# Four up-projection groups of an MLP as seven block products, with the MLP's program order computed from a task plan

## The chip, the cores and the metric

The kernel runs on one core of one Trainium2 chip. The metric is device time in microseconds (us), the median of several executions. Five engines work side by side, each going through its own instructions in program order and waiting on semaphores for the others: TensorE (PE in the profile, with its weight loads shown apart as PEld), VectorE (DVE), ScalarE (ACT), GpSimd (POOL) and SyncE (SP). SP issues nearly all loads and stores; POOL issues the DMAs that add into their destination.

## The reference, cut to what matters

One decoder layer on 512 tokens of width 1024: two mixing branches, a merge, and then a squared-ReLU MLP of width 4096. The change is in the MLP, the last lines:

```
x  = x + jnp.einsum('bsd,de->bse', merged, w_out[l])
h2 = rmsnorm(x, norm_mlp_g[l])
up = jnp.square(jax.nn.relu(jnp.einsum('bsd,df->bsf', h2, w_up[l])))
x  = x + jnp.einsum('bsf,fd->bsd', up, w_down[l])
```

## The kernel before, in words

**Precision.** Every large product is made of three: both operands are split into a high part (ACT copies the float32 value into the rounded type, `fp32r`) and a low part (DVE subtracts the high part from the value), and `high*high + high*low + low*high` goes into one PSUM bank. A weight block of 128 x 1024 so costs one load on SP, one ACT cast (tile `whi`) and one DVE subtraction (tile `wlo`). There are five pairs of `whi`/`wlo` buffers, four in the pool `wp` and one in `fin`, so the weights can lead the products by at most five blocks (`slots`, `weight_pair`, L80 to 84). Four buffers hold raw blocks: two of tag `rx` and two of tag `wraw` (`load`, L1036).

**The MLP's work.** The list of its products starts at L1004, the loop over them at L1284. `w_up` is cut into 8 groups of 512 hidden columns and `w_down` into 8 matching pieces; the work goes in 4 chunks `d`. Chunk `d` does up group `2d`, up group `2d+1`, then the two halves `(d, 0)` and `(d, 1)` of the down projection. The list `steps` holds the products in this order. A group is done in one of two ways:

- **Plain** (`"pl"`: groups 0, 1, 3, 5 and 7): four weight blocks `b0`, `b2`, `b1`, `b3`, each used by 8 x 3 matmuls of 128 x 512, 96 matmuls in all.
- **Seven products** (`"up"`: groups 2, 4, 6, and every down half, `"dn"`): the 2 x 2 block product is done with seven block products `M1` to `M7` instead of eight (a Strassen-Winograd form), in the order M1, M5, M6, M2, M7, M3, M4. Each product is 24 matmuls of 128 x 256, 168 in all. Sums of weight blocks and of activation blocks are needed for it, and sums of results behind it.

The weight sums are made in two ways. For groups 2, 4 and 6 they are computed long before the MLP with adding DMAs on POOL and kept in DRAM (`weight_sums`, L281, tiles `up2M...`), so these groups load seven finished blocks. For the down halves four blocks are loaded, DVE adds twice in place (`plus`, L1063, `raw<-raw`: for M5 and M6), and POOL adds twice with a DMA (in `cast_lo`, L1086, `raw<-raw`: for M7 and M4). The text calls a group whose sums are made on the spot a *grown* group.

**Banks.** A seven-product group uses three PSUM banks X, Y and Z. M1, M6, M7 and M4 all go into Y, one onto the other, with a copy or an addition of the state by ACT or DVE between them; M5 and M3 share Z. So one product lies between two products of the same bank, and what takes the first one's result has to be done in that time.

**After the products.** `plain_out` and `up_out` (L1157 to 1228) make relu and square on ACT, the four sums of activation blocks on DVE (`total`), and high and low parts of the seven forms (tiles `us`). `down_out` (L1230) adds each down product into `x` on DVE; in the last chunk it scales and stores the rows.

**The order by hand.** Matmuls, DVE, ACT and POOL instructions are chained in the order in which the program emits them (`InOrder`, L59). The loop over `steps` emits a product, then one weight step (`ahead`, L1104: the subtraction of one block and the cast of the next). Work behind a product is delayed with `later(us, f)` (L1120) and let go by `tick` (L1123), with hand-written delays such as `later(4.9, ...)`. At the start of each down half `(d, 0)` stands one extra matmul of 64 columns, whose result the next one overwrites:

```
if kind == "dn" and a[1] == 0 and p == "M1" and k == 0:
    I.matmul((b[0] if isinstance(b, tuple) else b)[:, :64], hi[:, 0, :P], forms[2 * a[0]][:, 0, f, 0, :64], start=True, stop=True)
```

**Lines in the profile.** Nearly every instruction goes through `InOrder` and so has line L67; the tile names tell the work apart: `acc<-h,...` is an up product, `acc<-us,...` a down product, `x<-acc,x` the addition of a down product, `q<-acc,...` the work behind an up product, `fs` the activation sums, `us<-...` their high and low parts.

Of the kernel before, what the change touches and what calls it, by code (L numbers as in the profile page):

```python
# [19 lines left out]
P = 128  # L20
# [17 lines left out]
def tile_block(ctx: ExitStack, tc: tile.TileContext, x, w_in, w_rga, w_rgx, w_pa, w_pr, w_o,  # L38
# [935 lines left out]
    def merged(j):  # L974
        def done(ps):
            q = fin.tile([P, 4, 256], F32, tag="q", name="q")
            d = h2[:, :, j]
            for c in range(2):
                t = 2 * j + c
                V.tensor_tensor(out=x2[:, t, :], in0=ps[c], in1=x2[:, t, :], op=ALU.add)  # L980
                A.activation(q[:, 2 * c:2 * c + 2], x2[:, t, :].rearrange("p (u s) -> p u s", u=2), AF.Copy, scale=smt[:, C_G2 + t:C_G2 + t + 1])
            for c in range(2):
                hi_part(d[:, :, 2 * c:2 * c + 2], q[:, 2 * c:2 * c + 2])
                lo_part(d[:, :, 2 * c:2 * c + 2], q[:, 2 * c:2 * c + 2])
            def sums():
                fs = fin.tile([P, 4, 256], F32, tag="fs", name="fs")
                sums_to(fs, *(q[:, m] for m in (1, 0, 3, 2)))
                hi_part(d[:, :, 4:8], fs)
                late.append(lambda: lo_part(d[:, :, 4:8], fs))
# [11 lines left out]
    FORM = {"M1": 0, "M4": 1, "M2": 2, "M5": 3, "M6": 4, "M7": 5, "M3": 6}  # L1001
    ORDER7 = ("M1", "M5", "M6", "M2", "M7", "M3", "M4")
    every = range(4)
    steps = []  # L1004

    def products(kind, a, order=ORDER7, first=3, lead=()):
        steps.extend((kind, a, p, q) for q in (range(first), range(first, 4)) for p in lead)
        steps.extend((kind, a, p, every) for p in order if p not in lead)

    I = InOrder(nc.tensor)  # L1010
# [10 lines left out]
    uses = {"M1": ("b0",), "M5": ("b0", "b1"), "M6": ("b0", "b3"), "M2": ("b2",), "M7": ("b1", "b3"), "M3": ("b3",), "M4": ("b2", "b0")}  # L1021
    loads = []
    for kind, a, p in ops:
        if kind == "pl":
            loads.append(((kind, a, p), w_up[a, int(p[1])]))
        elif kind == "up":
            loads.append(((kind, a, p), w_up[a, int(uses[p][0][1])] if p in ("M1", "M2", "M3") else summed[a // 2 - 1][p]))
        else:
            b = w_dn[2 * a[0] + a[1]].rearrange("a b p c -> (a b) p c")
            for q in (0, 1, 3, 2) if a[1] else (0, 2, 1, 3):  # L1030
                if p == "M1":
                    loads.append((("dn", a, f"b{q}"), b[q]))
    raw, dead, units, half = {}, set(), [], []
    n_load, n_free, n_low = [0], [0], [0]

    def load():  # L1036
        while n_load[0] < min(len(loads), n_free[0] + 4):
            n = n_load[0]
            if n >= 2 and len(wb.raw) < len(wb.reqs):
                break  # L1040
            what, src = loads[n]
            t = fin.tile([P, 4, 256], F32, tag="rx", name="raw", bufs=2) if n % 4 < 2 else wp.tile([P, 4, 256], F32, tag="wraw", name="raw", bufs=2)
            nc.sync.dma_start(t, src.rearrange("p (k c) -> p k c", k=4))
            raw[what] = t
            n_load[0] += 1

    def drop(what):
        dead.add(what)
        while n_free[0] < n_load[0] and loads[n_free[0]][0] in dead:
            n_free[0] += 1  # L1050
        load()

    def can_cast():
        load()
        n = len(units)
        if n == len(ops) or slots[0] == 0:
            return False
        kind, a, p = ops[n]
        return all((kind, a, q) in raw for q in (uses[p] if kind == "dn" else (p,)))

    added, cast = set(), set()

    def plus(n):  # L1063
        if n in added or n >= len(ops):
            return
        kind, a, p = ops[n]
        if kind == "dn" and p in ("M5", "M6"):
            x, y = (raw.get((kind, a, q)) for q in uses[p])
            if x is None or y is None:
                return  # L1070
            V.tensor_tensor(out=x, in0=x, in1=y, op=ALU.add)
        added.add(n)

    def cast_hi():
        n = len(units)
        plus(n)
        slots[0] -= 1
        kind, a, p = ops[n]
        src = raw[kind, a, uses[p][0] if kind == "dn" else p]
        own = n % 5 == 4  # L1080
        hi, lo = weight_pair((0 if own else 64) if kind != "pl" else 192 if own else 0, fin if own else None)
        A.copy(hi, src)
        units.append((hi, lo))
        half.append((hi, lo, src, ops[n]))

    def cast_lo(more=True):  # L1086
        hi, lo, src, (kind, a, p) = half.pop(0)
        V.tensor_tensor(out=lo, in0=src, in1=hi.bitcast(F32), op=ALU.subtract)
        n_low[0] += 1
        if kind != "dn":  # L1090
            drop((kind, a, p))
        elif p in ("M2", "M6"):
            cast.add((a, p))
            if {(a, "M2"), (a, "M6")} <= cast:
                G.dma_start(raw[kind, a, "b2"], raw[kind, a, "b0"], accum_op=ALU.add)
                drop((kind, a, "b0"))
        elif p in ("M7", "M3", "M4"):
            drop((kind, a, uses[p][0]))
        if kind == "dn" and p == "M5":
            G.dma_start(raw[kind, a, "b1"], raw[kind, a, "b3"], accum_op=ALU.add)  # L1100
        if not half and more:
            plus(len(units))

    def ahead():  # L1104
        if half:
            cast_lo()
        if can_cast():
            cast_hi()

    finished, freed = set(), [0]  # L1110

    def finish(o):
        finished.add(o)
        while freed[0] < len(ops) and ops[freed[0]] in finished:
            freed[0] += 1
            slots[0] += 1

    clk, due = [0.0], []

    def later(us, f):  # L1120
        due.append((clk[0] + us, f))

    def tick(us):  # L1123
        clk[0] += us
        for d in sorted(due, key=lambda d: d[0]):
            if d[0] <= clk[0]:
                due.remove(d)
                d[1]()

    two = lambda b: b.rearrange("p (u s) -> p u s", u=2)  # L1130
    forms, quads = [None] * 8, {}

    def begin(n):
        if n % 2:
            t = fin.tile([P, 7168 + 64], F32R, tag="us1", name="us")[:, 48:48 + 7168]
        else:
            t = hp.tile([P, 7168], F32R, tag="hT", name="us")
        forms[n] = t.rearrange("p (r f h s) -> p r f h s", r=2, f=7, h=2)

    def squared(q, a, b, src=None):  # L1140
        A.activation(q[:, a:b], q[:, a:b] if src is None else src, AF.Relu)
        A.activation(q[:, a:b], q[:, a:b], AF.Square)

    def part(n, which, f0, f1, src, u=slice(0, 2)):
        return lambda: which(forms[n][:, :, f0:f1, u], src)

    def total(n, fs, *ms, u=slice(0, 2)):
        q = quads[n][0][:, :, u]
        fs = [f[:, :, u] for f in fs]
        for m in ms:  # L1150
            x, y, op = ((q[:, 0], q[:, 2], ALU.subtract), (fs[0][:, 0], q[:, 1], ALU.subtract), (q[:, 1], q[:, 0], ALU.subtract), (q[:, 3], fs[0][:, 1], ALU.add))[m]
            V.tensor_tensor(out=fs[m // 2][:, m % 2], in0=x, in1=y, op=op)

    def rests():
        return hp.tile([P, 2, 2, 256], F32, tag="tail", name="fs"), fin.tile([P, 2, 2, 256], F32, tag="fs", name="fs")

    def up_out(n, p, X, Y, Z):  # L1157
        if p == "M1":
            begin(n)
            snap = fin.tile([P, 2, 256], F32, tag="fs", name="snap")  # L1160
            A.copy(snap, two(Y))
            quads[n] = fin.tile([P, 4, 2, 256], F32, tag="q", name="q"), snap
            return
        q, snap = quads[n]
        if p == "M5":
            A.copy(q[:, 2], two(Z))
        elif p == "M6":
            A.copy(q[:, 3], two(Y))
        elif p == "M2":
            V.tensor_tensor(out=q[:, 1], in0=two(X), in1=snap, op=ALU.add)  # L1170
            later(1.0, lambda: squared(q, 1, 2))
# [19 lines left out]
    def plain_out(n, c, u, ps):  # L1191
# [12 lines left out]
        if u == 0:  # L1204
            quads[n] = q, rests()
# [44 lines left out]
    def sums2():  # L1250
        split(s2[:, 0], s2[:, 1], ssq)
# [134 lines left out]
```

## Time and profile before

| what | value |
|---|---|
| time, median of 3 runs | 851.39 us (850.86 to 852.13) |
| span of the profiled execution | 849.3 us |
| PE, PEld, DVE, ACT, POOL busy | 843.4, 762.0, 632.1, 460.7, 97.0 us |
| first MLP product starts, last one ends | 523.80, 845.37 us |
| granted TensorE clock | 1.000 |

The span runs from the first to the last instruction of one profiled execution. A matmul's row shows its start and a modelled duration that overlaps the next one's; the pace of PE is read from the distance of starts, or from how long a stage with a known number of matmuls takes. The same holds for DVE and ACT to a smaller degree: instructions back to back start a little sooner than the shown duration says. A figure in brackets behind a row is the idle time in front of it, with what ended it.

### The profile page before, as it was taken

Reading aid. Unit: us, or ns where it says so; the run is one execution under the profiler, and the core shown is the slowest. Engines: PE = TensorE matmul, PEld = TensorE weight load, DVE = VectorE, ACT = ScalarE, POOL = GpSimd, SP = SyncE. Lnnn points to the kernel's source line nnn. Section 1 sums busy time; section 2 is a strip of 40 time slices with the busy share of each in tenths; the row PEclk is TensorE's granted clock in tenths of the full one; section 3 lists DMA queues with packets and bytes.
Section 4 is the critical chain, followed back from the end, with each engine's and each line's share of the span. In section 5 each row is a group of like instructions: output and inputs, shape, how many; then the busy total and the mean of one; then the engine's idle time right before and its main releaser. Section 6 shows DMA issues by size and latency. Waiting matters only on the chain.

```text
span 849.3 us, 13700 instructions
## 1 busy us (share of the span) xinstructions
PE 843.4 (99%) x5395; PEld 762.0 (90%) x5395; DVE 632.1 (74%) x1061; ACT 460.7 (54%) x719; POOL 97.0 (11%) x124
## 2 busy tenths in 40 slices
PE   9999999999999999999999999999999999999998
PEld 7899999999888888888888888889999998999898
DVE  6766788888877246878875767698786858876797
ACT  7445465655655336577662456563466356545641
POOL 0041232313211101111111000000000000000000
PEclk9999999999999999999999999999999999999999
DMA  5356332343332346686656651414843565356354
GB/s 202 123 158 205 106 94 71 94 124 88 87 93 77 99 151 189 188 231 175 187 152 188 223 215 45 157 38 137 248 149 77 150 221 149 124 153 198 98 149 124
DMA packets 40016, 121.85 MB, mean 143 GB/s; under 512 B 4864, under 2 KB 9672, under 8 KB 39952
## 3 DMA queue, kind: packets, MB, share of 16 engines
q1 hardware_dynamic: 31152, 92.65, 33.2%
q0 software_dynamic: 8800, 28.33, 15.2%
q8 instruction: 42, 0.69, 0.3%
q14 instruction: 22, 0.18, 0.1%
HBM read 102.05 MB, written 11.05 MB: 133 GB/s over the span
## 4 chain that ended last, share of the span: by engine, by line
PE 94%; DVE 4%; ACT 1%; issue 1%; DVEq 0%
PE acc L67 38%; PE acc L137 15%; PE acc L138 15%; PE acc L139 15%; PE at L593 2%; PE at L137 2%; PE at L138 2%; PE at L139 2%; PE at L629 1%; DVE wlo L67 1%; PE at L527 1%; PE at L666 1%; DVE pe L67 1%; DVE hT L67 0%; DVE xT L67 0%
## 5 line engine op out<-in xcount | busy, mean ns | idle before, releaser
L67 PE MATMUL acc<-h,whi 128*128 128x512 f32 (+1 forms) x656 | 156.5, 332 | 0.0
L67 PE MATMUL acc<-us,whi 128*128 128x256 f32 (+1 forms) x900 | 154.1, 277 | 0.1
L67 DVE TENSOR_TENSOR wlo<-wraw,whi 128x1024 fp32r<-128x1024 f32 (+2 forms) x86 | 96.9, 1148 | 71.9 <-ACT whi L67 68.7
L67 ACT CAST whi<-raw 128x1024 fp32r<-128x1024 f32 x97 | 99.7, 1049 | 91.4 <-DVE raw L67 41.1
L67 PEld LDWEIGHTS acc<-us,whi 128*128 128x128 f32 x900 | 136.1, 188 | 0.6 <-DVE x L67 0.3
L67 DVE TENSOR_TENSOR wlo<-raw,whi 128x1024 fp32r<-128x1024 f32 x97 | 117.5, 1218 | 15.4 <-ACT whi L67 15.2
L67 PE MATMUL acc<-us,wlo 128*128 128x256 f32 x448 | 124.0, 277 | 0.0
L67 PEld LDWEIGHTS acc<-h,whi 128*128 128x128 f32 x656 | 110.9, 188 | 12.3
L67 PE MATMUL acc<-h,wlo 128*128 128x256 f32 (+1 forms) x328 | 108.9, 332 | 0.0
L67 ACT CAST whi<-wraw 128x1024 fp32r<-128x1024 f32 (+2 forms) x86 | 82.5, 982 | 48.5 <-DMA wraw<-in_w_in_dram 31.7
L137 PE MATMUL acc<-whi,hT 128*128 128x256 f32 x384 | 108.4, 282 | 0.0
L138 PE MATMUL acc<-wlo,hT 128*128 128x256 f32 x384 | 107.3, 279 | 0.2 <-DVE wlo L67 0.2
L67 PEld LDWEIGHTS acc<-us,wlo 128*128 128x128 f32 x448 | 84.1, 188 | 0.0
L137 PE MATMUL acc<-hT,whi 128*128 128x512 f32 x208 | 81.7, 393 | 0.0
L139 PE MATMUL acc<-hT,wlo 128*128 128x512 f32 x208 | 81.0, 390 | 0.0
L139 PE MATMUL acc<-whi,hT 128*128 128x256 f32 x288 | 80.3, 279 | 0.0
L138 PEld LDWEIGHTS acc<-wlo,hT 128*128 128x128 f32 x384 | 72.4, 189 | 0.6 <-DVE wlo L67 0.4
L137 PEld LDWEIGHTS acc<-whi,hT 128*128 128x128 f32 x384 | 72.4, 188 | 0.5 <-issue 0.2
L67 ACT ACTIVATE pe<-pe,nm 128x128 f32<-128x128 f32 (+3 forms) x64 | 35.6, 558 | 65.9 <-DVE nm L67 65.9
L67 PEld LDWEIGHTS acc<-h,wlo 128*128 128x128 f32 x328 | 61.6, 188 | 6.3
L138 PE MATMUL acc<-hT,whi 128*128 128x512 f32 x156 | 60.8, 390 | 0.0
L67 POOL TENSOR_TENSOR rs<-ms,mhalf 128x8 f32<-128x8 f32 (+1 forms) x25 | 39.4, 1579 | 187.2 <-DVE ms L67 187.2
(210 smaller groups left out, 1680.2 us busy)
## 6 DMA issues: line engine op xcount, KB each, us to landing
wraw<-in_w_in_dram SPq DMA_DIRECT2D x54, 512.0 KB, 3.6
raw<-in_w_dn_dram SPq DMA_DIRECT2D x32, 512.0 KB, 4.1
raw<-in_w_up_dram SPq DMA_DIRECT2D x29, 512.0 KB, 4.3
sum<-in_w_up_dram POOLq DMA_DIRECT2D x18, 512.0 KB, 5.7
raw<-raw POOLq DMA_DIRECT2D x16, 512.0 KB, 4.6
wraw<-in_w_pa_dram SPq DMA_DIRECT2D x8, 512.0 KB, 4.6
wraw<-in_w_pr_dram SPq DMA_DIRECT2D x8, 512.0 KB, 3.6
wraw<-in_w_o_dram SPq DMA_DIRECT2D x8, 512.0 KB, 4.7
```

Source lines behind the costliest of these rows:

```text
L67: ins = f(*a, **k)
L137: T.matmul(o, l[0], r[0], start=first, stop=False)
L138: T.matmul(o, l[0], r[1], start=False, stop=False)
L139: T.matmul(o, l[1], r[0], start=False, stop=last)
L527: T.transpose(out=ps[:, t * P:(t + 1) * P], in_=qn[t // 2][:, c0:c0 + P], identity=ident)
L593: T.matmul(lg[c][:, :N], qT[:, c, i * P:(i + 1) * P], qk[h % 2, z][:, c, :N], start=z == 1, stop=z == 2)
L629: T.transpose(out=tp[:, b * P:(b + 1) * P], in_=st[s][:, b * P:(b + 1) * P], identity=ident)
L666: T.matmul(ps[:, t:t + 1], sq[:, t * P:(t + 1) * P], ones, start=True, stop=True)
```

## The change

Groups 1, 3, 5 and 7 become seven-product groups of a third kind, `"uq"`: grown like the down halves, from four loaded blocks of `w_up`, two DVE additions and two adding DMAs on POOL. `FORM`, `ACT8` and the banks are those of the other seven-product groups. Group 0 stays plain. In a down half `(d, 0)` the products M2, M5 and M6 are cut in two, first the part over group `2d`'s forms, then that over group `2d+1`'s:

```diff
-        products("pl", 2 * d + 1, ("b0", "b2", "b1", "b3"))
-        products("dn", (d, 0))
+        products("uq", 2 * d + 1)
+        products("dn", (d, 0), ("M1",))
+        steps.extend(("dn", (d, 0), p, q) for q, ps in (((0, 1), ("M2", "M5", "M6")), ((2, 3), ("M6", "M2", "M5"))) for p in ps)
+        products("dn", (d, 0), ("M7", "M3", "M4"))
         products("dn", (d, 1))
```

The hand-written order of the MLP goes (`ahead`, `cast_hi`, `cast_lo`, `plus`, `drop`, `finish`, `later`, `tick`, `up_out`, `plain_out`, `down_out`). In its place every load, cast, subtraction, addition, product and post-processing step is a `Task` with an engine, a length in us and the tasks that it comes after:

```
LOAD, SUM, HOP, TRIES = 4.4, 4.9, 0.06, 400
AFTER = {"PE": 0.17, "DVE": 0.09, "ACT": 0.09}
dve = lambda columns: 0.08 + 0.00105 * columns
act = lambda columns: 0.1 + 0.00085 * columns
```

The weight steps of a grown group (the order of POOL's two additions and their target differ from before: M4's sum goes into block 0):

```
l = [load_task(w[q], b[q]) for q in range(4)]
m1 = unit("M1", w[0], l[0])
s5 = grow("DVE", w[0], w[1], m1, l[1])
m5 = unit("M5", w[0], s5)
s7 = grow("POOL", w[1], w[3], s5, l[3])
s6 = grow("DVE", w[0], w[3], m5, l[3])
m6 = unit("M6", w[0], s6)
s4 = grow("POOL", w[0], w[2], m6, l[2])
unit("M2", w[2], l[2])
unit("M7", w[1], s7)
unit("M3", w[3], l[3])
unit("M4", w[0], s4)
```

While the program is built on the host, a list scheduler (`lay_out`) places the tasks on the engines by due times, which are counted back from an ideal sequence of products; 400 random variations of the ranks are tried, and the layout whose last product ends soonest is kept. The tasks are then emitted in order of their planned starts, which fixes each engine's program order and the raw buffer of each load; at run time only the semaphores wait. The order of PE's products is that of `steps` in any layout:

```
for t in sorted((t for t in plan if t not in begun), key=lambda t: t.start):
    if t in tags:
        t.go(tags[t])
    else:
        t.go()
```

Smaller edits: the tile `q` of four quarters becomes four tiles `q0` to `q3`; the two `rx` buffers become `ra` and `rb`, and a load takes any free one of the four raw buffers; the last high part of the sums of `h2` (`late`, j = 3) moves behind the merge; the reciprocal, the scaling of `x` and the final scaled rows are tasks like the others. The 64-column matmul stays at the start of every `(d, 0)`:

```
if kind == "dn" and a[1] == 0 and p == "M1" and u.start == 0:
    I.matmul((banks[b][0] if split_y else banks[b])[:, :64], hi[:, 0, :P], forms[2 * a[0]][:, 0, f, 0, :64], start=True, stop=True)
```

More of the change, by code (lines that the diff above doesn't have):

```diff
@@ L1001, in tile_block, with products @@
     FORM = {"M1": 0, "M4": 1, "M2": 2, "M5": 3, "M6": 4, "M7": 5, "M3": 6}
+    ACT8 = {"M1": 0, "M4": 3, "M2": 2, "M5": 4, "M6": 5, "M7": 6, "M3": 7}
+    BANK = {"M2": "X", "M5": "Z", "M3": "Z"}
     ORDER7 = ("M1", "M5", "M6", "M2", "M7", "M3", "M4")
-    every = range(4)
+    every = (0, 1, 2, 3)
     steps = []
[L1006 to L1010, printed above, removed]
+    def products(kind, a, order=ORDER7):
+        steps.extend((kind, a, p, every) for p in order)
     for d in range(4):
@@ L1033, in tile_block, with __init__ @@
[L1033 to L1042, printed above, removed]
+    class Task:
+        def __init__(self, engine, us, go, after, land):
+            self.engine, self.us, self.go, self.after, self.land = engine, us, go, list(after), us + land
+            self.then, self.start, self.due, self.raw, self.frees = [], None, None, None, []
@@ L1061, in tile_block @@
[L1061 to L1128, printed above, removed]
@@ L1248, in tile_block @@
[L1248 to L1260 removed]
+        t = task("SP", 0.1, go, (), LOAD)
@@ new lines, in load_task, with cast_task, go, low_task @@
+        t.raw = what
+        users[what] = [t]
+        return t
+    def cast_task(o, what, after):
+        n = number[o]
+        def go():
+            place = places[n % len(places)]
+            own = place == "fin"
+            units[o] = weight_pair((0 if own else 64) if o[0] != "pl" else 192 if own else 0, fin if own else None)
+            A.copy(units[o][0], raw[what])
+        t = task("ACT", act(1024), go, after)
+        users[what].append(t)
+        return t
+    def low_task(o, what, after):
+        def go():
+            hi, lo = units[o]
+            V.tensor_tensor(out=lo, in0=raw[what], in1=hi.bitcast(F32), op=ALU.subtract)
+        t = task("DVE", dve(1024), go, after)
+        users[what].append(t)
+        return t
@@ new lines, in tile_block, with load @@
+    done_at = {}
+    s2 = hp.tile([P, 2, S], F32R, tag="tail", name="s2")
+    I = InOrder(nc.tensor)
+    ready = [lambda: casts[ops[0]].go()]
+    for n in range(3):
+        ready.append(lambda n=n: (lows[ops[n]].go(), casts[ops[n + 1]].go()))
+    first = [t for t in plan if t.raw][:4]
+    n_ready = [0]
+    def load():
+        while first and (len(first) > 2 or len(wb.raw) == len(wb.reqs)):
+            t = first.pop(0)
+            t.start = -20.0
+            tag = ("ra", "rb", "wraw", "wraw")[3 - len(first)]
+            buffers[tag].append(t.raw)
+            del buffers[tag][0]
+            t.go(tag)
@@ L1262, in tile_block, with ahead @@
+    def ahead():
+        load()
+        if slots[0] > 0 and ops[n_ready[0]] in raw:
+            slots[0] -= 1
+            ready[n_ready[0]]()
+            n_ready[0] += 1
     for j in range(4):
@@ L1279, in tile_block @@
         late.pop(0)()
[L1280 to L1296 removed]
+    sum3 = task("DVE", 4 * dve(256), owing.pop(0))
@@ new lines, in tile_block, with bank_task, norm_go @@
+    free_at = {}
+    state = {}
+    def bank_task(key, us, go, after, fresh):
+        if fresh:
+            seq.append(key)
+            if len(seq) > 8:
+                after = list(after) + queue[seq[-9]]
+        else:
+            after = list(after) + queue.get(key, [])
+        return task("PE", us, go, after)
+    def norm_go():
+        ps = banks["norm"] = psum("acc")
+        for z in range(2):
+            I.matmul(ps, onesr.broadcast_to([P, P]), s2[:, z], start=z == 0, stop=z == 1)
@@ new lines, in tile_block @@
+            free_at[o] = pe
+            continue
+        if (kind, a) not in state:
+            state[kind, a] = {}
+        b = kind, a, BANK.get(p, "Y")
+        split_y = kind == "dn" and a[0] == 3 and b[2] == "Y"
+        fresh = b not in queue
+        after = [lows[o]]
+        if kind == "dn":
+            after += [x for i in pairs for x in made[2 * a[0] + i // 2, FORM[p]]]
+        elif a == 1 and p in ("M5", "M6", "M7", "M3"):
+            after.append(low3)
+        end = 3 in pairs
@@ new lines, in tile_block @@
+        queue[b] = posts
+        if end:
+            free_at[o] = pe
+        if kind == "dn" and a[1] == 1:
+            last_of_chunk[a[0]] = pe
+    for n, o in enumerate(ops):
+        if n >= len(places):
+            join(casts[o], free_at[ops[n - len(places)]])
+        if n:
+            join(casts[o], casts[ops[n - 1]])
+    clk = 0.0
+    for t in plan:
+        if t.engine == "PE":
+            t.ideal = clk
+            clk += t.us
+    began = [t for t in plan if t.start is not None]
```

559 lines of the change are left out of this document (352 added, 207 removed).

## The prediction

> **What bounds the kernel now.** I read the page first (busy shares, the chain), then the granted clock, then a table of stretches with one row for each group of the MLP, and last the timelines of PE, DVE and ACT around the places where those rows differ.
>
> ```profile
> PE 843.4 (99%) x5395; PEld 762.0 (90%) x5395; DVE 632.1 (74%) x1061; ACT 460.7 (54%) x719; POOL 97.0 (11%) x124
> ...
> PE 94%; DVE 4%; ACT 1%; issue 1%; DVEq 0%
> ```
>
> PE is the bound: 99% busy and 94% of the chain that ends last. A busy PE need not be a fast PE, though, so the pace is read from stages. In the table below each row is one group of the MLP: first the single plain group 0 with the normalising matmuls, then pairs of rows that hold 96 matmuls of 512 columns (plain) or 168 of 256 columns (seven products). Columns: length, then busy time of PE, PEld, DVE, ACT, POOL, then clock, DMA share, GB/s.
>
> ```profile
> 523.80:546.03 22.23, 22.23 (x100) 18.40 (x98) 15.36 (x20) 15.05 (x22) 0.00 (x0) 1.00 0.51 157
> ...
> 666.62:686.40 19.78, 19.78 (x170) 19.78 (x169) 14.44 (x16) 8.46 (x9) 0.86 (x1) 1.00 0.67 176
> 686.40:706.19 19.79, 19.79 (x171) 19.79 (x169) 12.28 (x13) 11.78 (x15) 0.00 (x0) 1.00 0.59 197
> 706.19:727.98 21.79, 21.79 (x99) 18.02 (x98) 15.37 (x18) 14.13 (x20) 0.86 (x1) 1.00 0.35 97
> 727.98:747.14 19.16, 19.16 (x171) 19.16 (x170) 17.52 (x25) 9.18 (x13) 1.72 (x2) 1.00 0.47 143
> 747.14:766.18 19.04, 19.04 (x171) 19.04 (x170) 14.04 (x16) 9.16 (x9) 0.86 (x1) 1.00 0.68 187
> 766.18:785.22 19.04, 19.04 (x171) 19.04 (x169) 12.18 (x13) 11.11 (x14) 0.00 (x0) 1.00 0.63 197
> ...
> 826.16:845.40 19.24, 19.20 (x170) 19.01 (x168) 16.85 (x29) 4.96 (x5) 0.86 (x1) 1.00 0.50 133
> ```
>
> A plain group takes 21.79 us. A seven-product group takes 19.04 us, but two of them (666.62 and 686.40) take 19.78, at the same clock of 1.00 and with PE shown as wholly busy. So there are two paces for the same 168 matmuls: 19.04/168 = 113.3 ns and 19.78/168 = 117.7 ns each. The timeline of PE shows where the slower one begins and where it can begin:
>
> ```profile
> 657.75 0.28 PE L67 MATMUL acc<-us,wlo 128*128 128x256 f32 x1
> 658.15 0.50 PE L67 MATMUL acc<-us,whi 128*128 128x256 f32 x2
> ...
> 663.26 0.28 PE L67 MATMUL acc<-us,wlo 128*128 128x256 f32 x1
> ...
> 663.60 0.28 PE L67 MATMUL acc<-us,wlo 128*128 128x256 f32 x1
> 663.71 0.48 PE L67 MATMUL acc<-us,whi 128*128 128x256 f32 x2
> 664.02 0.28 PE L67 MATMUL acc<-us,wlo 128*128 128x256 f32 x1
> 664.14 0.40 PE L67 MATMUL acc<-us,whi 128*128 128x256 f32 x2
> 664.38 0.28 PE L67 MATMUL acc<-us,wlo 128*128 128x256 f32 x1
> ```
>
> Up to 663.60 a triple of matmuls takes 0.34 us; the pair at 663.71 lasts 0.48 instead of 0.39, a slip of 0.09 us, and behind it a triple takes 0.36 (664.02 to 664.38). By the table it stays so to 706.19, until a plain group comes. The longer wait at 657.75 to 658.15 (0.29 over the usual 0.11) was not followed by the slow pace. Two more kinds of place set the pace:
>
> ```profile
> 41.04 0.28 PE L137 MATMUL acc<-whi,hT 128*128 128x256 f32 x1
> 41.16 0.28 PE L138 MATMUL acc<-wlo,hT 128*128 128x256 f32 x1
> 41.27 0.28 PE L139 MATMUL acc<-whi,hT 128*128 128x256 f32 x1
> 41.39 0.28 PE L137 MATMUL acc<-whi,hT 128*128 128x256 f32 x1
> ```
>
> Here, straight behind matmuls of 512 columns, the first of 256 come every 0.117 us, the slow pace. In the MLP the 64-column matmul stands at that place; it costs 19.16 − 19.04 = 0.12 us (row 727.98 against 747.14), and the fast pace follows it.
>
> **What the change removes on PE.** The four groups 1, 3, 5 and 7 fall from 21.79 to 19.04: 4 x 2.75 = 11.0 us, all on the path, if they run at the fast pace. I take the whole MLP anew, against this execution. Before, it ran on PE from 523.80 to 845.40: 321.6 us. After: group 0 with its normalising matmuls 22.23, fifteen seven-product groups at 19.04 (285.6), four 64-column matmuls (0.5), and 0.2 for the last group's end (row 826.16 against 747.14): 308.5. That is 13.1 less: 11.0 from the products, 1.6 from the slow stretch (two rows at +0.74 and a little of the one before), the rest from the waits at 658.15 and 663.71. The span of 849.3 becomes 836.2. The profiled execution stands 2.1 below the median of the runs; I carry that along: 838.3 us is the floor, with every matmul at the fast pace and no wait.
>
> **What is added to it on PE.** Group 1 now follows the normalising matmuls of 512 columns, and no 64-column matmul stands there: as at 41.04 I give it the slow pace, +0.74. For the other fourteen groups the pace is the unknown. Before, each chunk had a plain group in it, which ended a slow stretch; after, nothing but the 64-column matmul (once in four groups) or a longer wait can. It now follows 256-column matmuls, which no row shows; I bound it between "always sets the fast pace" (0) and "does nothing or sets the slow one" (14 x 0.74 = 10.4 us). The trace had one lasting slip in eleven groups, with a DVE that had more room than it will have. I take five slow groups of the fourteen, 3.7 us, nearer to the first end since all four 64-column matmuls were followed by the fast pace. Waits of the size at 658.15, one a chunk: 4 x 0.3 = 1.2.
>
> **What is added elsewhere, and what hides it.**
>
> ```profile
> L67 DVE TENSOR_TENSOR raw<-raw 128x1024 f32<-128x1024 f32 x16 | 19.6, 1224 | 0.7 <-DMA raw<-in_w_dn_dram 0.3
> L67 ACT CAST whi<-raw 128x1024 fp32r<-128x1024 f32 x97 | 99.7, 1049 | 91.4 <-DVE raw L67 41.1 <-DMA raw<-raw 27.9 <-PE acc L67 7.1
> L67 ACT COPY snap<-acc 128x512 f32<-128x512 f32 x3 | 1.8, 587 | 8.2 <-PE acc L67 8.2
> L67 PEld LDWEIGHTS acc<-us,whi 128*128 128x128 f32 x900 | 136.1, 188 | 0.6 <-DVE x L67 0.3
> ...
> 657.41 0.68 DVE L67 TENSOR_TENSOR x<-x,acc 128x512 f32<-128x512 f32 x1
> 658.01 1.22 DVE L67 TENSOR_TENSOR wlo<-raw,whi 128x1024 fp32r<-128x1024 f32 x1
> 659.15 0.69 DVE L67 TENSOR_TENSOR fs<-q,fs 128x512 f32<-128x512 f32 x1
> ```
>
> Back to back a 512-column DVE instruction takes 0.60 us (657.41 to 658.01) and a 1024-column one 1.14. A grown up group has three more subtractions, two additions of raw blocks (5 x 1.14 = 5.7) and three combinations of banks (3 x 0.60 = 1.8): 7.5 us more on DVE, four times. ACT gets three casts and three copies: 3 x 1.05 + 3 x 0.59 = 4.9. In chunk 2 (rows 686.40 to 747.14) DVE had 12.28 + 15.37 + 17.52 + 14.04 = 59.2 us of work, ACT 44.3; after, 66.7 and 49.2 in 76.3 us. So neither is the bound over a chunk. But over the grown up group and the first down half DVE gets 15.37 + 17.52 + 7.5 = 40.4 us of work in 19.04 + 19.16 = 38.2. The 2.2 us too many have to be done ahead: the even up group leaves DVE 19.04 − 12.28 = 6.8 free, and five weight buffers let the weights lead by four products, 4 x 19.04/7 = 10.9 us, less a cast and a subtraction, about 8.6. I price it at no wait for weights, and at the 1.2 of small waits above: a DVE that waits for an ACT cast holds the bank additions queued behind it, PE's next product in that bank waits for those, and such a slip is what costs the pace.
>
> ```profile
> raw<-in_w_up_dram SPq DMA_DIRECT2D x29, 512.0 KB, 4.3
> ...
> raw<-raw POOLq DMA_DIRECT2D x16, 512.0 KB, 4.6
> ```
>
> Loads from DRAM stay four a group (4.3 us each). On POOL eight adding DMAs come new, 4.6 us to landing; POOL has nothing else in these stages (0.86 to 1.72 busy in a row). SP's order is now planned, so a load that waits for a raw buffer holds the loads behind it, as before. One buffer's round in a grown group, from rows: load 4.3, three casts and subtractions for M1, M5, M6 with two additions between them (3 x 2.19 + 2 x 1.14 = 8.9), the casts of M2 and M7 with the latter's subtraction (1.05 + 2.19 = 3.2), then block 1's buffer is free: 16.4 us, under the 19.04 that PE takes. M4's sum now starts right behind M6's subtraction, not behind M2's too. Cutting `q` in four, the late high part of `h2`, which group 1's M5 needs a whole plain group (21.8 us) later, the moved reciprocal and final scaling: no cost, all beside PE; the end after the last product (849.3 − 845.4 = 3.9) stays, for nothing else is left on DVE then.
>
> A rule of the Trainium skill speaks against the change: the page "TensorE: Matmul & The Clock Gate", section "The mechanism", says that weight loads overlap running matmuls only where they use different row groups; by it 72 more weight loads a group would stand bare. The row 747.14 of the table disagrees: PEld and PE are both busy for all 19.04 us. By that section's rule, with the load's 107 ns that the section "LDWEIGHTS (loading the stationary operand)" gives (my estimate: 72 x 0.107 = 7.7 us more a group), the change would lose 4 x (7.7 − 2.75) = 20 us; by the row it gains.
>
> Sum: 838.3 + 0.74 + 3.7 + 1.2 = 843.9 us.
>
> **The rivals.** *Fast throughout*: the 64-column matmuls set the pace and the planned order avoids slips: 838.3 + 0.7 to 2 of the rest, about 839.5. For it: four of four such matmuls before. *Slow throughout*: what is saved goes back as pace: 838.3 + 11.1 + 1.2 = 850.6. For it: one slip of 0.1 us held for over two groups; against: longer waits end it. *Starved of weights*, the one that ends slower:
>
> ```profile
> 659.01 1.05 ACT L67 CAST whi<-raw 128x1024 fp32r<-128x1024 f32 x1 [2.23 <-DMA raw<-in_w_dn_dram]
> ...
> 678.22 1.05 ACT L67 CAST whi<-raw 128x1024 fp32r<-128x1024 f32 x1 [5.29 <-DMA raw<-raw]
> 681.92 2.95 ACT L67 CAST whi<-raw 128x1024 fp32r<-128x1024 f32 x3 [2.65 <-DMA raw<-in_w_up_dram]
> ...
> 695.57 2.00 ACT L67 CAST whi<-raw 128x1024 fp32r<-128x1024 f32 x2
> ```
>
> The down half (1, 1) had its first cast at 659.01, the group behind it at 681.92: 22.9 us for one grown group, with 5.3 of them waiting for POOL's sum, against 19.04 on PE. The even up group needs only 14.6 (681.92 to 696.5). Three grown groups in a row would lose 3 x 3.9 − 4.4 = 7.3 us a chunk, 29 in all: 867. It turns slower than before when a grown group takes over some 21.6 us ((3.3 + 4.4)/3 above 19.04, with 13.1/4 = 3.3 a chunk to lose). Against it: the 16.4 us above. *Bare weight loads*, a mechanism that would put each added matmul's load of 188 ns on the path: 72 x 4 x 0.188 = 54 us, and 892 in all; the page named above states it, and the row 747.14 gives it no chance.
>
> **How the numbers follow.** Forecast 0.53 (840.5 to 847.5), fast throughout 0.20, slow throughout 0.14 (847.5 to 852), starved 0.13 (of it 0.03 under 849.7), bare loads 0. About 0.2%, 1.7 us, is what a measurement of this kernel can tell: faster means under 849.7, slower over 853.1. Faster: 0.53 + 0.20 + half of the slow case 0.07 + 0.03 = 0.83; same 0.07 + 0.02 = 0.09; slower 0.08. The range leaves out what lies above 850.0, some 0.16, and almost nothing below 838.5.
>
> **What would show it.** Right: matmuls of 128x512 on `acc<-h` fall from 480 to 96, PE's count rises by 288; `raw<-raw` 24 times on DVE and on POOL; stage rows of 19.04 or 19.78 with nothing between but small waits; group 1 at 19.78. Wrong: rows above 20 us with PE idle and casts that wait for `raw<-raw` (starved), or slow rows in more than nine groups.

## The result, and the profile after

The changed kernel takes 845.17 us (median of 8 runs, 843.87 to 849.53) against 851.65 (8 runs, 850.14 to 853.90) of the kernel before: a ratio of 0.9928, with a 95% interval of 0.9907 to 0.9950. The profiled execution took 845.48, its span is 843.6. From the page of the changed kernel, busy times and the chain:

```profile
PE 837.0 (99%) x5683; PEld 769.4 (91%) x5683; DVE 655.9 (78%) x1077; ACT 478.1 (57%) x753; POOL 103.9 (12%) x132
...
PE 91%; DVE 6%; DMA 2%; issue 1%; ACT 1%; SPq 0%; DVEq 0%
```

PE is still the bound, with 288 matmuls more and 6.4 us less. The table of stretches, one row a group, columns as before the change: group 0, group 1, the down halves (0, 0) and (0, 1), then (1, 0), group 5, (2, 0), (2, 1) and (3, 1).

```profile
524.90:547.15 22.25, 22.25 (x99) 18.39 (x98) 19.42 (x24) 15.95 (x28) 1.76 (x2) 1.00 0.36 95
547.15:566.20 19.05, 19.05 (x170) 19.04 (x168) 18.76 (x24) 16.81 (x26) 0.86 (x1) 1.00 0.64 166
566.20:585.91 19.71, 19.62 (x171) 19.44 (x170) 19.71 (x26) 9.48 (x12) 1.72 (x2) 1.00 0.55 146
585.91:604.95 19.04, 19.04 (x170) 19.04 (x169) 17.67 (x19) 8.95 (x9) 0.86 (x1) 1.00 0.54 154
...
643.13:663.36 20.23, 19.89 (x172) 19.57 (x170) 19.46 (x24) 11.00 (x15) 1.72 (x2) 1.00 0.53 147
...
701.44:720.48 19.04, 19.04 (x171) 19.04 (x169) 18.93 (x22) 16.64 (x24) 1.73 (x2) 1.00 0.63 167
720.48:740.37 19.89, 19.89 (x171) 19.89 (x170) 18.38 (x23) 10.13 (x14) 1.72 (x2) 1.00 0.54 141
740.37:760.16 19.79, 19.79 (x170) 19.79 (x169) 14.22 (x16) 8.10 (x8) 0.86 (x1) 1.00 0.69 196
...
819.63:839.58 19.95, 19.95 (x170) 19.74 (x168) 16.89 (x28) 4.94 (x5) 0.86 (x1) 1.00 0.50 127
```

Group 1 takes 19.05 where the plain one took 21.8. Up to 720.48 the undisturbed groups run at 19.04; from (2, 0) to the end every one takes 19.8 to 19.95, with PE shown as busy throughout. The timeline of PE has both events, the start of (0, 0) and a wait in it:

```profile
566.08 0.28 PE L69 MATMUL acc<-h,wlo 128*128 128x256 f32 x1
566.20 0.51 PE L69 MATMUL acc<-us,whi 128*128 128x64 f32 x3
566.54 0.28 PE L69 MATMUL acc<-us,wlo 128*128 128x256 f32 x1
...
566.90 0.28 PE L69 MATMUL acc<-us,wlo 128*128 128x256 f32 x1
...
571.84 0.28 PE L69 MATMUL acc<-us,wlo 128*128 128x256 f32 x1
572.21 0.48 PE L69 MATMUL acc<-us,whi 128*128 128x256 f32 x2
...
572.88 0.28 PE L69 MATMUL acc<-us,wlo 128*128 128x256 f32 x1
...
573.22 0.28 PE L69 MATMUL acc<-us,wlo 128*128 128x256 f32 x1
```

Behind the 64-column matmul (first of the three merged in row 566.20) a triple takes 0.36 us (566.54 to 566.90): the slow pace, in a stream that was fast before it. Behind the wait at 572.21 a triple takes 0.34 (572.88 to 573.22): fast again. What PE waited for stands on DVE:

```profile
569.65 1.22 DVE L69 TENSOR_TENSOR wlo<-raw,whi 128x1024 fp32r<-128x1024 f32 x1
570.78 0.68 DVE L69 TENSOR_TENSOR fs<-fs,q 128x512 f32<-128x512 f32 x1
571.38 0.68 DVE L69 TENSOR_TENSOR x<-acc,x 128x512 f32<-128x512 f32 x1
```

M1 of (0, 0) ended at 569.1, but its addition (`x<-acc,x`) had a subtraction and an activation sum ahead of it on a DVE without a gap; it ended at 572.06, and M6, which goes into the same bank, started at 572.21. The counts are those of the change: `raw<-raw` 24 times, 64 + 32 matmuls of 512 columns left on `acc<-h`:

```profile
L69 DVE TENSOR_TENSOR raw<-raw 128x1024 f32<-128x1024 f32 x24 | 29.3, 1219 | 0.6 <-DMA raw<-in_w_up_dram 0.4
...
L69 PE MATMUL acc<-h,whi 128*128 128x512 f32 x64 | 19.7, 390 | 0.0
L69 PE MATMUL acc<-h,wlo 128*128 128x512 f32 x32 | 12.4, 389 | 0.0
```

### The profile page after: what moved, and what is told of

Its sections match the earlier page's. It is cut to its first block, busy times and chain, and to the rows that moved or that the text cites. A ratio compares the mean times of both kernels' runs of the same rounds, so it can differ in the third digit from the quotient of the medians.

```text
span 843.6 us, 14367 instructions
## 1 busy us (share of the span) xinstructions
PE 837.0 (99%) x5683; PEld 769.4 (91%) x5683; DVE 655.9 (78%) x1077; ACT 478.1 (57%) x753; POOL 103.9 (12%) x132
## 4 chain that ended last, share of the span: by engine, by line
PE 91%; DVE 6%; DMA 2%; issue 1%; ACT 1%; SPq 0%; DVEq 0%
PE acc L69 34%; PE acc L139 16%; PE acc L140 16%; PE acc L141 16%; PE at L595 2%; DVE wlo L69 2%; PE at L139 2%; PE at L141 2%; PE at L140 2%; PE at L631 1%; PE at L529 1%; DMA wraw<-in_w_in_dram 1%; DMA raw<-in_w_dn_dram 1%; PE at L668 1%; DVE pe L69 0%
## 5 line engine op out<-in xcount | busy, mean ns | idle before, releaser
L69 ACT CAST whi<-raw 128x1024 fp32r<-128x1024 f32 x109 | 111.6, 1047 | 87.7 <-DVE raw L69 29.8
L69 PE MATMUL acc<-us,whi 128*128 128x256 f32 (+1 forms) x900 | 156.9, 279 | 0.4 <-DVE x L69 0.3
L69 PE MATMUL acc<-h,whi 128*128 128x256 f32 (+1 forms) x848 | 154.8, 286 | 0.0
L69 DVE TENSOR_TENSOR wlo<-raw,whi 128x1024 fp32r<-128x1024 f32 x109 | 131.0, 1219 | 19.8 <-ACT whi L69 19.7
L69 PEld LDWEIGHTS acc<-h,whi 128*128 128x128 f32 x848 | 130.7, 188 | 2.6
L69 PE MATMUL acc<-h,wlo 128*128 128x256 f32 (+1 forms) x424 | 121.2, 286 | 0.0
L139 PE MATMUL acc<-hT,whi 128*128 128x512 f32 x208 | 81.7, 393 | 0.0
L69 PEld LDWEIGHTS acc<-h,wlo 128*128 128x128 f32 x424 | 79.6, 188 | 1.3
L69 POOL DMA_DIRECT2D raw<-raw x24 | 20.7, 864 | 330.2 <-DVE wlo L69 72.4
```

The lines of the kernel that those rows point to most:

```text
L69: ins = f(*a, **k)
L139: T.matmul(o, l[0], r[0], start=first, stop=False)
```

## The experiments

All times are medians. Each ratio is to the kernel before as it ran on the same chip in the same series (medians 850.65 to 851.65), so kernels of different series are best compared by their ratios. The last three columns are of the profiled execution and count the MLP's 256-column matmuls by their distance, the time from one start to the next: those with 116 to 120 ns are slow, and cost what is above 113.3 ns; what a distance of over 122 ns has above 113.3 is put down as a wait. Below, a stretch is called fast or slow by its distances, and the pace is said to be drawn anew where either pace may follow.

| kernel | us (range, runs) | ratio to before, 95% | its profile, us | slow matmuls, their cost | waits, us |
|---|---|---|---|---|---|
| before | 851.65 (850.14 to 853.90, 8) | | 849.3 span | 365, 1.6 | 0.8 |
| after | 845.17 (843.87 to 849.53, 8) | 0.9928, 0.9907 to 0.9950 | 845.5 | 1114, 5.0 | 1.6 |
| no64 | 842.26 (840.78 to 849.88, 12) | 0.9921, 0.9897 to 0.9946 | 848.6 | 2303, 10.3 | 0.7 |
| before_no64 | 857.70 (856.14 to 858.04, 4) | 1.0073, 1.0060 to 1.0086 | 857.5 | 1070, 4.8 | 1.0 |
| plan_plain | 854.66 (853.42 to 855.38, 5) | 1.0044, 1.0031 to 1.0057 | 853.4 | 476, 2.1 | 2.6 |
| one64 | 849.68 (1) | | 849.7 | 2302, 10.3 | 0.7 |
| m2whole_no64 | 848.74 (844.09 to 850.79, 9) | 0.9955, 0.9935 to 0.9975 | 845.7 | 1294, 5.8 | 1.8 |
| m2whole_64 | 847.20 (845.40 to 849.61, 4) | 0.9950, 0.9931 to 0.9969 | 847.1 | 1347, 6.0 | 2.4 |
| pair | 843.53 (841.27 to 844.19, 5) | 0.9907, 0.9893 to 0.9921 | 841.3 | 128, 0.6 | 2.0 |
| m2whole_pair | 845.29 (841.10 to 847.65, 6) | 0.9920, 0.9899 to 0.9941 | 845.7 | 1165, 5.2 | 1.7 |
| pair_late | 846.77 (844.66 to 848.47, 8) | 0.9942, 0.9920 to 0.9964 | 846.8 | 655, 2.9 | 4.5 |
| pair_no_search | 848.00 (846.82 to 852.08, 12) | 0.9964, 0.9947 to 0.9982 | 846.8 | 288, 1.3 | 6.8 |
| pair_load60 | 849.36 (845.39 to 854.02, 12) | 0.9985, 0.9966 to 1.0005 | 850.1 | 475, 2.1 | 7.4 |
| pair_load52 | 845.87 (843.72 to 848.29, 6) | 0.9940, 0.9920 to 0.9960 | 847.5 | 1231, 5.5 | 1.9 |

The theory behind the prediction (A): PE's work falls by the products, and what is lost of that is pace and small waits. The rivals are named with each run.

The profiles give the account by which the runs can be read. Take the MLP's time on PE and subtract the last two columns. What is left, the matmuls at the fast pace, is 319.0 to 319.1 us in before, before_no64 and plan_plain, and 307.9 to 308.1 in after, no64, one64, m2whole_no64 and m2whole_64: 11.0 us less, the 4 x 2.75 of the prediction, whatever the order of the other engines. By the way the columns are counted, whatever else differs on PE stands under pace or waits, so this says what the products save and not what causes the rest; the runs are for that.

**no64** and **one64**: what sets the slow pace?

```diff
-            if kind == "dn" and a[1] == 0 and p == "M1" and u.start == 0:
-                I.matmul((banks[b][0] if split_y else banks[b])[:, :64], hi[:, 0, :P], forms[2 * a[0]][:, 0, f, 0, :64], start=True, stop=True)
```

> The changed kernel without the four 64-column matmuls at the start of the down halves (d, 0); nothing is left out of the computation, since the next matmul overwrites their result. Theory A (a 64-column matmul inside a stream of 256-column ones sets the slow pace): the stream stays at 113.3 ns, the groups from (2, 0) on take 19.04 instead of 19.79 us, and the time falls by 6.3 x 0.75 + 4 x 0.12 = 5.2 us, to about 840. Theory B (the slow pace of the last two chunks comes from the fuller DVE, ACT and DMA, whatever stands there): the groups from (2, 0) on stay at about 19.8 us, and the time falls by at most 0.5 us.

```diff
-            if kind == "dn" and a[1] == 0 and p == "M1" and u.start == 0:
+            if kind == "dn" and a == (1, 1) and p == "M1" and u.start == 0:
```

> The changed kernel with a single 64-column matmul, in front of M1 of the down half (1, 1) instead of the four; nothing is left out of the computation. Theory A: the triples of 256-column matmuls take 0.34 us up to that matmul and 0.353 behind it, from (1, 1) to the end or to a wait of some 0.3 us; about 9.5 groups x 0.75 = 7 us above the kernel without any. Theory B: the pace changes elsewhere, not at that place.

Seven of the twelve runs of no64 lie at 840.8 to 842.5, as A expects, and five at 847.0 to 849.9. The profile fell among the latter; its PE timeline:

```profile
570.22 0.28 PE L69 MATMUL acc<-us,wlo 128*128 128x256 f32 x1
...
570.56 0.28 PE L69 MATMUL acc<-us,wlo 128*128 128x256 f32 x1
571.24 0.47 PE L69 MATMUL acc<-us,whi 128*128 128x256 f32 x2 [0.41 <-ACT us L69]
571.55 0.28 PE L69 MATMUL acc<-us,wlo 128*128 128x256 f32 x1
...
571.91 0.28 PE L69 MATMUL acc<-us,wlo 128*128 128x256 f32 x1
```

Fast up to a wait of 0.6 us in front of M6 of (0, 0), slow from there to the end (triples of 0.36), 2303 matmuls. The row names an ACT cast that ended at 571.15; M1's bank addition on DVE, which M6 needs, ended at 571.10 beside it. B falls: seven runs are over 2 us below the 844.7 that it allowed at the least, and in the profiled run chunk 3 is no slower than chunk 0. But A in its simple form falls too: a wait can start the slow pace as well as end it. None of the seven was profiled; that they keep the fast pace is concluded from their time. Over all fourteen profiles, of the 26 distances of 0.3 us or more that began in a fast stretch and whose pace behind them can be told, 13 were followed by the fast pace and 13 by the slow. one64 had the same wait at 571.39 and was slow long before its 64-column matmul, so it tells nothing about that.

**before_no64**: is it that matmul that kept the kernel before fast?

```diff
-        if kind == "dn" and a[1] == 0 and p == "M1" and k == 0:
-            I.matmul((b[0] if isinstance(b, tuple) else b)[:, :64], hi[:, 0, :P], forms[2 * a[0]][:, 0, f, 0, :64], start=True, stop=True)
```

> The kernel before, without the four 64-column matmuls; nothing is left out of the computation. Theory A with its other half (straight behind 512-column matmuls the 256-column ones start at the slow pace, and there the 64-column matmul sets the fast one): the seven-product groups that now take 19.04 us take 19.79, about 9 groups x 0.75 - 0.5 = 6 us more, some 858 us. Theory B: 851 us, within 0.5.

```profile
570.84 0.39 PE L67 MATMUL acc<-h,wlo 128*128 128x512 f32 x1
571.07 0.40 PE L67 MATMUL acc<-us,whi 128*128 128x256 f32 x2
571.30 0.28 PE L67 MATMUL acc<-us,wlo 128*128 128x256 f32 x1
...
571.66 0.28 PE L67 MATMUL acc<-us,wlo 128*128 128x256 f32 x1
...
572.01 0.28 PE L67 MATMUL acc<-us,wlo 128*128 128x256 f32 x1
```

857.70, 6.2 us up on the before of the same chip (851.54). Straight behind the plain group's last 512 columns the triples take 0.36 and 0.35 us; the profile shows this at all four places. In chunk 0 it lasts until the next plain group and in chunk 3 to the end; in chunk 1 a slip of 0.08 us ends it (663.52), in chunk 2 a wait of 0.24 us (746.64). So the same instruction helps behind 512 columns.

**plan_plain**: the task plan without the products.

```diff
-        products("uq", 2 * d + 1)
-        products("dn", (d, 0), ("M1",))
-        steps.extend(("dn", (d, 0), p, q) for q, ps in (((0, 1), ("M2", "M5", "M6")), ((2, 3), ("M6", "M2", "M5"))) for p in ps)
-        products("dn", (d, 0), ("M7", "M3", "M4"))
+        products("pl", 2 * d + 1, ("b0", "b2", "b1", "b3"))
+        products("dn", (d, 0))
...
-            if p == "b3":
+            if p == "b3" and a == 0:
```

> The task plan alone: groups 1, 3, 5 and 7 plain again and the down halves (d, 0) uncut, with the 64-column matmuls behind plain groups as before. If the saving is the products' alone (theory A): 849 to 851 us, the plan being worth only the waits at 658.15 and 663.71 and the slow stretch behind them, at most 2.1 us. Theory C (the plan carries most of the gain, by feeding PE better): 845 to 847 us.

854.66, 3.1 us slower than the hand-written order; C falls, and the 849 to 851 of theory A is missed too. Part of that is waits, which stand at one place in three chunks, M5 of (d, 0), which uncut needs the odd group's activation sums; on PE and DVE:

```profile
571.36 0.28 PE L69 MATMUL acc<-us,whi 128*128 128x256 f32 x1
572.12 0.38 PE L69 MATMUL acc<-us,whi 128*128 128x256 f32 x1 [0.48 <-DVE us L69]
```

```profile
571.38 0.68 DVE L69 TENSOR_TENSOR us<-fs,us 128x512 fp32r<-128x512 f32 x1
```

The low part ends at 572.06, and PE goes on. The three waits are 1.9 us of the 2.6 in the table, and they come with the uncut half. On top of this plan the products with their cut halves are worth 854.66 − 845.17 = 9.5 us; since the changed kernel does not have these waits, not all of the 9.5 is saved columns. Plain groups with cut halves were not tried.

**m2whole_no64**, **m2whole_64**: take the wait in front of M6 away by another order of PE's products.

```diff
-        products("dn", (d, 0), ("M1",))
-        steps.extend(("dn", (d, 0), p, q) for q, ps in (((0, 1), ("M2", "M5", "M6")), ((2, 3), ("M6", "M2", "M5"))) for p in ps)
+        products("dn", (d, 0), ("M1", "M2"))
+        steps.extend(("dn", (d, 0), p, q) for q, ps in (((0, 1), ("M5", "M6")), ((2, 3), ("M6", "M5"))) for p in ps)
```

> No 64-column matmuls, and in the down halves (d, 0) M2 is no longer cut: M1, M2 whole, then the halves M5, M6 of the even forms and M6, M5 of the odd ones, so that 1.4 us more lie between M1 and M6, which share a bank. Theory D (PE waits for the addition of M1's result on a full DVE, and any such wait draws the pace anew, often the slow one): the wait of 0.6 us in front of M6 goes, all fifteen groups run at 19.04 us, and the runs lie close together at 840 to 841, without the upper cluster of 847 to 850 that the kernel without 64-column matmuls has. Rival E (the pace is drawn by something else, once per run): the same two clusters as there, and waits elsewhere.

> The same order with M2 whole, but with the four 64-column matmuls. Theory A/D (inside a 256-column stream the 64-column matmul sets the slow pace, and here no wait sets it back): slow from (0, 0) to the end, fourteen groups x 0.75 + 0.5 = 11 us above the kernel with M2 whole and without them, 851 to 852. Rival E: no more than 1 us above it.

D's forecasts both miss. The wait at that place goes, but the profile of m2whole_no64 has others of 0.3 to 0.5 us at 576.4, 734.9 and 759.8, in front of M7 and M4, which share the bank too. All three were followed by the fast pace. Its long slow stretch, 590.98 to 734.9, began with a slip of only 0.08 us, where the first matmul that needs the `wlo` of M6 of (0, 1) waited for DVE's subtraction; a second began with a slip of 0.04 us at 831.07. The median is 6.5 us above no64, though the intervals of the two ratios overlap. D's cure falls: on a full DVE the wait moved, and a slip far shorter than a wait can bring the slow pace. E's times fit better: two clusters again (844.1 to 846.0 and 848.7 to 850.8), though higher than those of no64, and m2whole_64 no slower than m2whole_no64. But its mechanism, one draw a run, does not fit, for the pace changes three times in this one profile. Of the 64-column matmuls of m2whole_64 two found a fast stretch and left a slow one, one found a slow one and left it slow, and the last found a slow one and left it fast.

**pair**, **m2whole_pair**, **pair_late**: put the 512 columns back in front.

```diff
             if kind == "dn" and a[1] == 0 and p == "M1" and u.start == 0:
+                I.matmul(banks[b][0] if split_y else banks[b], hi[:, 0, :P], forms[2 * a[0]][:, 0, f], start=True, stop=True)
                 I.matmul((banks[b][0] if split_y else banks[b])[:, :64], hi[:, 0, :P], forms[2 * a[0]][:, 0, f, 0, :64], start=True, stop=True)
```

> The changed kernel with a 512-column matmul in front of each of the four 64-column ones, so that these stand again behind 512 columns as in the kernel before; both results are overwritten. Theory A with its other half: the pair sets the fast pace at each of the four places, at 4 x 0.23 = 0.9 us; the waits in front of M6 in (0, 0) and (1, 0) draw it anew, and the pair of the next chunk mends that: 841 to 846. Rival E: as the changed kernel, 844 to 849.5, plus 0.9.

> M2 whole and the pair of a 512-column and a 64-column matmul at each (d, 0). Theory A/D: no wait in front of M6 and the fast pace set four times: 841 to 842.5, the runs close together. Rival E: spread over 5 us or more.

In pair_late the condition is `a[1] == 1`.

> The changed kernel with the pair of a 512-column and a 64-column matmul at the start of the down halves (d, 1) instead of the 64-column matmul at (d, 0). The wait in front of M6 of (d, 0) then lies shortly ahead of the pair. Theory F (after a wait the pace is drawn anew, the pair sets the fast one whatever went before): at most the rest of one (d, 0) is slow in a chunk, 0.6 us, so the profile shows fast groups from each (d, 1) on, and the time is 840.5 to 843, no higher than with the pair at (d, 0) (843.5). Rival G (the pair works only in a stream that is already fast): clusters as in the kernel without 64-column matmuls, up to 849.

The PE timeline of pair at (2, 0):

```profile
719.01 0.74 PE L69 MATMUL acc<-us,whi 128*128 128x512 f32 x4
719.58 0.28 PE L69 MATMUL acc<-us,wlo 128*128 128x256 f32 x1
...
719.92 0.28 PE L69 MATMUL acc<-us,wlo 128*128 128x256 f32 x1
...
720.26 0.28 PE L69 MATMUL acc<-us,wlo 128*128 128x256 f32 x1
```

Triples of 0.34 us behind it. Over all profiles a 64-column matmul behind 512 columns was followed by the fast pace 32 times of 32, whatever went before; in a fast 256-column stretch it was followed by the slow pace 5 times of 5. pair came out as expected, with the closest runs of all kernels with this change (5 runs within 2.9 us); m2whole_pair did not, for its waits undo the pair within the chunk, and its runs spread over 6.5 us, as E had it.

pair_late bears out F on the pair, which was followed by the fast pace all four times, and misses on the time: something else was late in that execution. In (2, 1) a wait of 2.4 us at 756.67 brought the slow pace back until the next pair at 821.5. DVE, ACT and PE of pair_late:

```profile
751.55 0.69 DVE L69 TENSOR_TENSOR x<-acc,x 128x512 f32<-128x512 f32 x1 [0.28 <-PE acc L69]
757.25 1.22 DVE L69 TENSOR_TENSOR wlo<-raw,whi 128x1024 fp32r<-128x1024 f32 x1 [5.01 <-ACT whi L69]
758.39 0.68 DVE L69 TENSOR_TENSOR x<-x,acc 128x512 f32<-128x512 f32 x1
```

```profile
756.16 2.94 ACT L69 CAST whi<-raw 128x1024 fp32r<-128x1024 f32 x3 [6.15 <-DMA raw<-in_w_up_dram]
```

```profile
756.67 0.28 PE L69 MATMUL acc<-us,wlo 128*128 128x256 f32 x1
759.21 0.48 PE L69 MATMUL acc<-us,whi 128*128 128x256 f32 x2 [2.26 <-ACT whi L69]
```

A load issued at 749.99 landed at about 756.1, four loads being issued within 3 us. ACT's cast waits for it, DVE's subtraction for the cast, and behind that subtraction stands M7's bank addition (758.39), for which PE waits 2.4 us: one late load holds PE through two in-order queues. (PE's row names an ACT cast that ended at about the same time, 759.10; M4's own weights had been ready since 751.3.) Group 0 of this execution has 0.7 us of waits more, which the table does not count. Why its median is 3.2 us above pair's, with the busy time of DVE, ACT and POOL the same within 0.4 us, is not settled by one profile.

**pair_no_search**, **pair_load60**, **pair_load52**: what the plan's numbers are worth.

```diff
-    LOAD, SUM, HOP, TRIES = 4.4, 4.9, 0.06, 400
+    LOAD, SUM, HOP, TRIES = 4.4, 4.9, 0.06, 0
```

> The pair at the start of (d, 0), and the first layout of the plan taken without the 400 random variations; PE's order of products is the same, only the order on DVE, ACT, POOL and SP differs. Theory H (the variations remove waits that the first layout leaves): PE waits of several us more, 847 or above. Rival I (the due times alone feed PE): the same as with the search, 843.5 within 1 us.

> The pair at the start of (d, 0), and the plan made with 6.0 us for a load instead of 4.4; only the order on DVE, ACT, POOL and SP changes. The rows show landings of 3.2 to 6.2 us, median 4.5. Theory J (what is left of the waits comes from orders that fit a median load and put a subtraction that needs the load ahead of a bank addition): PE's waits of 0.8 to 2.4 us go, 840 to 842.5. Rival K (an order planned with slower loads only moves the waits elsewhere, since DVE is full): 843 to 847.

> The same with 5.2 us for a load. Theory J: between the pair alone (843.5) and the plan with 6.0, 841 to 843.5. Rival K: anywhere within 843 to 847, and not in the order of the planned lengths.

H holds: without the variations the table has 6.8 us of waits instead of 2.0 (the longest 3.2 us at 590.2), and the time is 4.5 us more. Not all of the 6.8 is waiting: behind that long wait the granted TensorE clock fell to 0.5 for 3.4 us (594.4 to 597.8), and 14 matmuls that started 213 to 214 ns apart make up 1.4 us of it. The profile of pair_load60 has the same, 1.5 us of its 7.4, at 655.2 to 658.6 behind two waits of 1.0 and 1.5 us. J falls: planned with slower loads the order is worse, 845.87 at 5.2 and 849.36 at 6.0. K is right that the waits only move, but not on the numbers: 849.36 lies above its 843 to 847, and the times do go in the order of the planned lengths. No version clearly beats the changed kernel: no64 and pair lie lower, but the intervals of their ratios overlap with its own.

## Why the prediction was right, point by point

- **The floor.** Predicted 308.5 us for the MLP on PE without slow matmuls and waits; measured 839.58 − 524.90 = 314.68, less 5.0 and 1.6, is 308.1. (The 308.5 holds 0.5 for the 64-column matmuls, most of which the 1.6 holds here; without it 308.0 was predicted.) The term that carries the gain was right, and plan_plain shows that the products and not the plan are its source: without pace and waits its MLP takes 319.1 us, the same as before the change. With plain groups and uncut halves the plan costs 3.1 us; the prediction gave the plan nothing.
- **Group 1 slow (+0.74).** Wrong: 19.05 us. Behind the two normalising matmuls the fast pace came by itself, so the row 41.04 was not the nearest case.
- **The 64-column matmul.** This is the step that failed. I put its unknown effect near "always sets the fast pace", because it had done so four times behind 512 columns; inside a fast 256-column stretch it set the slow one, in all three cases of the changed kernel's profile and in both of m2whole_64. Of its bound, the end "does nothing or sets the slow one" was the right one for what the matmul does; the cost stayed below that end's 10.4 us because waits ended the slow stretches.
- **Pace in all.** 0.74 + 3.7 = 4.4 us predicted, 5.0 measured. That the size held is luck. The 0.74 was for a group that ran fast; the matmul set the slow pace more often than forecast; and a wait ended it after 46 matmuls in chunk 0, two slips in chunk 1 after some 60, which the prediction did not count on. It is also one draw: the other runs of the changed kernel lie between 843.87 and 849.53, and those of no64 in two clusters, up to 842.5 and from 847.0 on.
- **Waits.** 1.2 predicted beside 0.5 for the 64-column matmuls, together 1.7; measured 1.6, slips at these matmuls included. The mechanism was the one named, a bank addition behind weight work on a full DVE, and DVE's load was sized rightly: 66.3 us in chunk 2 (682.40 to 760.16), where 66.7 was predicted. DVE was busy 19.71 of 19.71 us in (0, 0), 18.76 of 19.05 in the group ahead of it.
- **Starved.** Did not come about, but the margin is thin: the subtraction for M6 of (0, 1) ended 0.5 us ahead of its product, that of (3, 1) 0.2 us. In m2whole_no64 the one for M6 of (0, 1) is 0.08 us late, and in pair_late a late load does reach PE. The bare weight loads did not show: PEld and PE are both busy for 19.04 us in the row 585.91.
- **Ahead of the MLP.** The MLP began 1.1 us later (524.90 against 523.80). The same program is already about 1.0 us later at 82 us, and in the profile of pair, which is the same program up to the MLP, it began at 523.92; that is the start-up of this execution and no part of the change. It makes up most of the distance between the profiled execution's 845.48 and the forecast of 843.9.
- **The 2.1 us carried along.** The prediction took them for a profiled execution that was faster than the median. Most of it is not that: in every execution on record the time is 1.7 to 2.0 us above the span. The step from span to time was right, its reason was not.

## What to carry to other kernels

Fewer matmul columns on the bound engine came back in full as work (11.0 us), but not as time: 6.5 us of it arrived, since the new order had more slow pace (5.0 us against 1.6) and more waits (1.6 against 0.8) than the old one. How much arrives depends on the slack that the engines which prepare the operands have stage by stage, and not only on average. When a group changes shape, look again at what stood beside it for the old shape: the 64-column matmul that set the fast pace behind 512 columns set the slow one in a fast stretch of 256. An engine that the profile shows as busy can be running at two paces, so read the distance of starts, stage by stage.

## What the runs showed of the hardware

Streams of 256-column `fp32r` matmuls, each with its own weight load, run at 113.3 or at 117.8 ns a matmul at a granted clock of 1.00, and keep either for hundreds of matmuls (2303 in no64). The pace is drawn at a disturbance:

- 512 columns straight in front of the 256 columns of a down product gave the slow one (4 of 4 in before_no64); the normalising matmuls of 512 columns in front of group 1's up products gave the fast one (11 of 11 profiles).
- A 64-column matmul between 512 and 256 columns gave the fast one (32 of 32), inside a fast 256-column stretch the slow one (5 of 5).
- A distance of 0.3 us or more gave either (13 fast, 13 slow), and shorter slips sometimes gave the slow one (663.71 in before, 590.79 and 831.07 in m2whole_no64).

What inside PE decides it is open. The length of a wait alone does not: the same distance of 0.76 us at the same place of plan_plain was followed by the slow pace in chunk 0 and by the fast one in chunks 1 and 2. The weight-load rows look alike at both paces (188 ns).

The granted clock is a separate matter, for both paces were seen at 1.00. In two profiles it fell to 0.5 for 3.4 us within about 1 us after PE had gone on from waits, one of 3.2 us (pair_no_search) and two of 1.0 and 1.5 us, 0.2 us apart (pair_load60); behind the single wait of 2.4 us in pair_late it stayed at 1.0.
